# A hybrid trunk layer: residual of the FFN added during the up products, value norm on ScalarE, another product order in the first pass

## The chip, the cores and the metric

The kernel runs on one core of one Trainium2 chip. The metric is the device time of one execution in microseconds; the time before is 2174.49 us, the median of 3 runs (2174.28 to 2175.36). The core has five engines with instruction queues of their own: TensorE (PE in the profile; PEld is its load of weights), VectorE (DVE), ScalarE (ACT), GpSimd (POOL) and SyncE (SP), which only issues DMAs here. Every queue is worked off in order. ScalarE and POOL issue DMAs too.

## What is computed

One layer of depth 1 over 2048 tokens of 1024 features, all in float32:

```python
h   = x @ w_in                                   # u | v | queries
z   = gelu(h[..., :2048]);  u = z[..., :1024]
v   = layer_norm(z[..., 1024:], v_g, v_b)
mix = u * (einsum('gij,bnjgc->bnigc', w_m, v) + b_s)
branch = concat([mix, memory_cross_attention(queries, mem, w_mem_kv)])
x = layer_norm(ALPHA * x + branch @ w_o, ln1_g, ln1_b)
x = layer_norm(ALPHA * x + (silu(x @ w_1) * (x @ w_2)) @ w_down, ln2_g, ln2_b)
```

Here `ALPHA` is 2 to the power of 1/4 and the FFN is 2816 wide. The term `ALPHA * x` of the last line is the residual of the FFN; the norm of `v` over its 1024 features is the norm that the change speaks of.

## The kernel before

**Precision and products.** Every float32 operand is split into a hi part (ScalarE, CAST, L73) and a lo part (VectorE, subtraction, L74), and each product is three matmuls (hi·hi, hi·lo, lo·hi). Larger products are made by a scheme of seven half-size products instead of eight: the sums of weights that products 3, 5, 6 and 7 need are made on VectorE (L132, L133, L135, L136 in `halves`), while products 1, 2 and 4 take raw pieces of the weights. Products 1 and 2 add up in bank q0, 5 and 3 in q2, 7 and 4 in q3, and 6 stands alone in q1. A tuple `ORDER` (L342, `1, 6, 5, 7, 2, 3, 4`) says in which order they are made.

**Order of work.** Each matmul is tied to the one before it (`in_order`), so TensorE's order is the program's. The instructions of the other engines are placed by a scheduler, which follows the program's order but moves an instruction ahead of others where it expects it to be ready.

**Mixer, 0 to about 745 us.** Four chunks of 512 tokens. `v_half` makes the value half: its matmuls, GELU on ScalarE (L694) into two tiles `z[0]` and `z[1]` of 128 x 4 x 512, statistics, an inverse square root in small VectorE steps (L319 to L324, result `rs`), and the norm: eight VectorE instructions a chunk over 128x512 (L702), which subtract the mean and multiply by `rs`. The gating products `sg` (`mixed`, L788) take `z` as their stationary operand: `mixed(0)` and `mixed(1)` use `z[0]`, the others `z[1]`. In chunk 0 the keys and values of the memory (`memory_kv`) and the queries (`queries`, products named `q`, weights `w_q`) follow `v_half`; in the other chunks the first quarter of `u` (`u_half`, products named `u`, weights `w_u`, sums L711 and L715) and the reading of the memory follow it. The weight sums of `u` and `q` are made on POOL. The layer norm behind the mixer centres in L226, squares in L229, scales in L280 and finishes in L289, and for the last chunk it runs inside the first steps of the FFN.

**FFN, three passes of 688, 680 and 680 tokens.** A pass has 22 steps `f`, each 128 of the 2816 columns, in five blocks. A step (`up`) is seven products of 12 matmuls each, named `h`. Behind each product stands its stage: a copy `m` of q0 on ScalarE behind product 1, sums on VectorE behind 6, 5, 7, 3 and 4 (L399, L400, L401, L391, L395), Silu on ScalarE, and the gating multiplications (L396, L397). A list `work` of generators is advanced once behind each stage: this is how other work (a norm, the splits of `g`, the sums of the down weights) is spread over the steps. The steps of a block are followed by its down projection, which adds to the accumulators `fa` (`pa.ya`). In the first pass all sums of weights are made from raw weights and kept in DRAM; the later passes read them back. In passes 1 and 2 the down projections of blocks 0 to 3 are `down7`: 4 pairs of output tiles with 28 products in all, named `e`, whose sums on VectorE are L523, L530 and L531. In the last of these four (`last`), `down7` also fetches the residual: 16 loads of 170 KB from `x1d` on SP's queue (L538) and 16 VectorE instructions of 128x340 that add it (L540). The step behind it begins with its weight `r_u`, loaded by SP (L141), and the split of its first product's weight, `w1`.

Of the kernel before, what the change touches and what calls it, by code (L numbers as in the profile page):

```python
# [11 lines left out]
F32 = mybir.dt.float32  # L12
F32R = mybir.dt.float32r
AF = mybir.ActivationFunctionType
# [3 lines left out]
P = 128  # L18
# [21 lines left out]
def trunk_kernel(ctx, tc, xT, memT, wv, wuq, ws, bs, vg, vb, wmk, wmv, wo,  # L40
# [304 lines left out]
    class Pass:  # L345
# [38 lines left out]
        def up(self, f, work):  # L384
            no, h = self.no, self.h
            name = f"{no}_{f}"
            q0, q1, q2, q3 = banks = [bank(f"h{i}_{name}")[:, 0:h] for i in range(4)]
            m1, u2, c12, c21, c22 = (self.tmp(f"{x}_{f}") for x in ("m1", "u2", "c12", "c21", "c22"))

            def sum3():  # L390
                nc.vector.tensor_add(c12, q2, u2)  # L391
                nc.scalar.activation(c12, c12, AF.Silu)

            def sum4():
                nc.vector.tensor_add(c21, q3, u2)  # L395
                nc.vector.tensor_mul(c22, c22, c12)  # L396
                nc.vector.tensor_mul(c21, c21, m1)  # L397

            stages = {1: lambda: nc.scalar.copy(m1, q0), 6: lambda: nc.vector.tensor_add(u2, q1, m1),  # L399
                      2: lambda: nc.scalar.activation(m1, q0, AF.Silu), 5: lambda: nc.vector.tensor_add(c22, q2, u2),  # L400
                      7: lambda: nc.vector.tensor_add(c22, q3, c22), 3: sum3, 4: sum4}  # L401

            def then(stage):
                def run():
                    stage()
                    for gen, times in work:
                        for _ in range(times):
                            next(gen, None)
                return run

            wab = w1[f], w1[NF + f], f"u{name}"
            left = plain(*wab) if no else halves(*wab, nc.vector, False)
            products(left, lambda p, k, b: self.x[p][k][:, b], banks,
                     name, {p: then(stage) for p, stage in stages.items()}, ORDER, 0, key=f"u{f}")
            return c21, c22

        def whole(self, f, ys):
# [83 lines left out]
        def down7(self, blk, q, f0, last, w):  # L501
# [23 lines left out]
            def second(j):  # L525
                for p in (2, 3, 4):
                    product(j, p)
                if last:
                    y, u = self.out[j], self.u[j]
                    nc.vector.tensor_add(y[:, 0, h:n], y[:, 0, h:n], u)  # L530
                    nc.vector.tensor_tensor(out=y[:, 1].rearrange("p (b t) -> p b t", b=2),  # L531
                                            in0=y[:, 1].rearrange("p (b t) -> p b t", b=2),
                                            in1=u.unsqueeze(1).broadcast_to([P, 2, h]), op=ALU.add)
                    for m in range(2):
                        m0 = (2 * j + m) * P
                        for x in range(2):
                            r, t0 = self.tmp(f"r{m}{x}_{j}"), self.t0 + x * h
                            nc.sync.dma_start(out=r, in_=x1d[m0:m0 + P, t0:t0 + h])  # L538
                            to = y[:, m, x * h:(x + 1) * h]
                            nc.vector.scalar_tensor_tensor(out=to, in0=r, scalar=ALPHA, in1=to,  # L540
                                                           op0=ALU.mult, op1=ALU.add)

            for j in range(KD // 2):
                if j < KD // 2 - 1:
# [4 lines left out]
                if j:  # L549
                    second(j - 1)  # L550
            second(KD // 2 - 1)

        def sums(self):

# [65 lines left out]
    class Chunk:  # L620
# [44 lines left out]
        def v_half(self, hooks):  # L665
# [31 lines left out]
                nc.vector.bn_aggr(mv[:, b, :], st[:, b])  # L697
            nc.vector.tensor_scalar(mv[:, :, 1], mv[:, :, 1], EPS, None, ALU.add)
            inv_sqrt(rs, mv[:, :, 1], rt)
            for h in range(2):  # L700
                for b in range(4):
                    nc.vector.tensor_scalar(z[h][:, b], z[h][:, b], mv[:, b, 0:1], rs[:, b:b + 1],  # L702
                                            ALU.subtract, ALU.mult)

        def feature_major(self, a, t, name, act):

# [195 lines left out]
    def run(c):  # L902
# [5 lines left out]
        if c == 0:  # L908
            for j in range(2):
                at(1, j, lambda j=j: load_memory(j))  # L910
            ch.v_half(hooks)
            memory_kv()
            gating_constants()
            ch.queries()
# [22 lines left out]
        else:  # L937
# [14 lines left out]
            ch.read(1)  # L952
            for j in range(3):
                ch.mixed(j)
                ch.gate(j)
                ch.u_half(j + 1)
            ch.mixed(3)
# [21 lines left out]
    late.norm.squares = open_pools["sq"]  # L979
    ffn.rest()  # L980
    norm_work = norm_steps([late.norm], [late.store], 5, 5)
    sums_to_make = [(blk, m) for blk in range(4) for m in range(0, KD, 2)]
    for no in range(len(FPASSES)):
        pa, h, n = ffn, FPASSES[no] // 2, FPASSES[no]
# [5 lines left out]
        side = []  # L990

        def up(f):
            work = [(norm_work, 1), *side]
            if no == 0 and f > 4 and sums_to_make:
                blk, m = sums_to_make.pop(0)
                work.append((pa.left_sums(blk, m, 4 * blk, 2), 1))
            ys = f, pa.up(f, work)
            for gen, _ in work[1:]:
                for _ in gen:
                    pass  # L1000
            side.clear()
# [2 lines left out]
        for blk, nb in enumerate(blocks):  # L1004
# [9 lines left out]
            else:  # L1014
                gs = [pa.whole(*y) for y in ahead] + [pa.whole(*up(f)) for f in fs]
                ahead = [] if end else [up(f0 + nb)]
            seven = no and not end
            if seven:
                first = [pa.left(blk, 0, f0, nb // 2)]
            if blk == 0:  # L1020
# [2 lines left out]
                pa.sums()  # L1023
            if seven:
                pa.down7(blk, nb // 2, f0, blk == len(blocks) - 2, first)
            elif not end:
                pa.down(blk, gs, f0, whole, lambda ci, m: None)
            elif no < len(FPASSES) - 1:
# [92 lines left out]
```

## Time and profile before

| | |
|---|---|
| median of 3 runs | 2174.49 us (2174.28 to 2175.36) |
| the profiled execution | 2181.2 us |
| its span, first to last instruction | 2179.4 us |
| mean granted TensorE clock | 0.984 |
| mixer / pass 0 / pass 1 / pass 2 and tail | about 0–752 / 752–1240 / 1240–1696 / 1696–2179 us |
| HBM traffic over the span | 186 GB/s |

Times in the views are in us from the span's start; a row of the timeline is start, length, engine, line, operation, output<-inputs by the program's names, shape and count, and in square brackets the idle time before it with what ended it. The granted clock is a share of full speed. Rows of a source line give the shortest, median and longest instruction in ns.

### The profile page before, as it was taken

Reading aid. Unit: us, or ns where it says so; the run is one execution under the profiler, and the core shown is the slowest. Engines: PE = TensorE matmul, PEld = TensorE weight load, DVE = VectorE, ACT = ScalarE, POOL = GpSimd, SP = SyncE. Lnnn points to the kernel's source line nnn. Section 1 sums busy time; section 2 is a strip of 40 time slices with the busy share of each in tenths; the row PEclk is TensorE's granted clock in tenths of the full one; section 3 lists DMA queues with packets and bytes.
Section 4 is the critical chain, followed back from the end, with each engine's and each line's share of the span. In section 5 each row is a group of like instructions: output and inputs, shape, how many; then the busy total and the mean of one; then the engine's idle time right before and its main releaser. Section 6 shows DMA issues by size and latency. Waiting matters only on the chain.

```text
span 2179.4 us, 35121 instructions
## 1 busy us (share of the span) xinstructions
PE 2095.6 (96%) x12938; PEld 1988.5 (91%) x12938; DVE 1591.2 (73%) x3050; ACT 921.9 (42%) x1846; POOL 350.7 (16%) x318
## 2 busy tenths in 40 slices
PE   9899999999999989999999999999999999999896
PEld 7898788788888889999999999999999999999895
DVE  6986796798789886778777875656748656666656
ACT  5553653564474453334334354232224353223234
POOL 0413321331322220011010330000002310000002
PEclk9999999999999999999999999999999999999998
DMA  6233314234333557667666557666754576667652
GB/s 213 78 109 122 118 62 161 97 107 142 129 97 108 171 202 262 246 243 267 233 249 252 175 198 267 222 228 236 265 203 147 194 274 224 233 229 235 236 167 88
DMA packets 155276, 408.13 MB, mean 187 GB/s; under 512 B 15584, under 2 KB 42336, under 8 KB 155104
## 3 DMA queue, kind: packets, MB, share of 16 engines
q1 hardware_dynamic: 132672, 325.80, 44.6%
q10 hardware_dynamic: 12672, 46.14, 5.5%
q0 software_dynamic: 9760, 33.95, 4.4%
q8 instruction: 102, 1.67, 0.3%
q14 instruction: 70, 0.57, 0.1%
HBM read 326.13 MB, written 79.69 MB: 186 GB/s over the span
## 4 chain that ended last, share of the span: by engine, by line
PE 63%; DVE 18%; DMA 7%; issue 5%; ACT 4%; POOL 3%; ACTq 0%; DVEq 0%; POOLq 0%; SPq 0%
PE h L60 31%; PE d L60 10%; PE e L60 9%; PE v L60 5%; PE u L60 3%; DMA r_x<-in_xT 2%; PE y L60 2%; DVE w_o L74 1%; DVE w L74 1%; DMA r_es<-in_w 1%; DMA r_u<-in_w 1%; DVE x L74 1%; POOL s_b L233 1%; DMA r_f<-x1d 1%; DVE w_u L74 1%
## 5 line engine op out<-in xcount | busy, mean ns | idle before, releaser
L60 PE MATMUL h<-x,w 128*128 128x340 f32 (+1 forms) x5544 | 891.7, 322 | 33.7 <-DVE w L74 24.9
L60 PEld LDWEIGHTS h<-x,w 128*128 128x128 f32 x5544 | 880.2, 190 | 40.9 <-DVE w L74 27.9
L60 PE MATMUL d<-g,w_d 128*128 128x344 f32 (+3 forms) x1632 | 260.8, 320 | 2.7 <-DVE w_d L74 1.6
L60 PEld LDWEIGHTS d<-g,w_d 128*128 128x128 f32 x1632 | 256.5, 188 | 5.1 <-DVE w_d L74 2.2
L60 PE MATMUL y<-br,w_o 128*128 128x512 f32 x960 | 224.2, 395 | 0.0
L60 PEld LDWEIGHTS y<-br,w_o 128*128 128x128 f32 x960 | 180.5, 188 | 41.8
L60 PE MATMUL e<-gp,w_e 128*128 128x340 f32 x1344 | 210.8, 317 | 0.0
L60 PEld LDWEIGHTS e<-gp,w_e 128*128 128x128 f32 x1344 | 209.7, 188 | 0.0
L73 ACT CAST w<-r_u 128x512 fp32r<-128x512 f32 x198 | 122.5, 619 | 194.0 <-PE h L60 96.6
L60 PE MATMUL v<-w_v,x 128*128 128x512 f32 x768 | 188.7, 402 | 6.5 <-ACT w_v L73 4.8
L60 PEld LDWEIGHTS v<-w_v,x 128*128 128x128 f32 x768 | 144.5, 191 | 41.9 <-ACT w_v L73 4.8
L74 DVE TENSOR_TENSOR w<-r_u,w 128x512 fp32r<-128x512 f32 x198 | 138.5, 702 | 24.7 <-ACT w L73 17.7
L391 DVE TENSOR_TENSOR c<-h,u 128x340 f32<-128x340 f32 (+1 forms) x66 | 33.7, 511 | 97.3 <-PE h L60 97.0
L60 PE MATMUL u<-xt,w_u 128*128 128x256 f32 x768 | 98.0, 284 | 0.0
L60 PEld LDWEIGHTS u<-xt,w_u 128*128 128x128 f32 x768 | 95.1, 192 | 0.0
L60 PE MATMUL u<-x,w_u 128*128 128x256 f32 x576 | 79.2, 290 | 11.2 <-DVE u L711 6.7
L60 PEld LDWEIGHTS u<-x,w_u 128*128 128x128 f32 x576 | 72.8, 193 | 13.7 <-issue 6.2
L74 DVE TENSOR_TENSOR w_o<-r_o,w_o 128x512 fp32r<-128x512 f32 (+1 forms) x96 | 67.0, 706 | 21.3 <-ACT w_o L73 21.1
L523 DVE TENSOR_TENSOR fa<-fa,e 128x340 f32<-128x340 f32 x128 | 63.6, 505 | 23.7 <-PE e L60 21.7
L73 ACT CAST w_d<-r_d 128x384 fp32r<-128x384 f32 (+2 forms) x104 | 53.2, 519 | 65.3 <-PE d L60 41.0
L73 ACT CAST w<-s_u 128x512 fp32r<-128x512 f32 x88 | 54.0, 618 | 58.2 <-PE d L60 33.4
L73 ACT CAST w_e<-r_e 128x256 fp32r<-128x256 f32 x96 | 35.9, 404 | 99.4 <-PE e L60 77.3
(212 smaller groups left out, 2837.5 us busy)
## 6 DMA issues: line engine op xcount, KB each, us to landing
w<-k_u SPq DMA_DIRECT2D x176, 512.0 KB, 4.0
r_u<-in_w SPq DMA_DIRECT2D x88, 512.0 KB, 3.6
k_u<-w ACTq DMA_DIRECT2D x88, 512.0 KB, 3.8
r_u<-in_wuq SPq DMA_DIRECT2D x32, 512.0 KB, 3.3
r_o<-in_wo SPq DMA_DIRECT2D x32, 512.0 KB, 3.5
r_e<-in_w SPq DMA_DIRECT2D x64, 256.0 KB, 3.5
w_e<-k_e SPq DMA_DIRECT2D x64, 256.0 KB, 3.8
w_e<-k_e SPq DMA_DIRECT2D x32, 512.0 KB, 4.5
```

What stands on the lines that cost most here:

```text
L60: in_order(nc.tensor.matmul(*args, **kw))
L73: nc.scalar.copy(hi, src)
L74: engine.tensor_sub(lo, src, hi.bitcast(F32))
L233: nc.gpsimd.tensor_add(self.s2, self.s2, sq)
L391: nc.vector.tensor_add(c12, q2, u2)
L523: nc.vector.tensor_add(to, to, bk)
```

## The change

Three things are changed, and the number of matmuls is the same.

First, `down7` no longer loads and adds the residual. A new generator `residual()` does it while the steps of blocks 1 and 2 run: it takes two tiles of the pool `ln` in turn, issues a load on POOL's queue (170 KB, 16 in a pass), waits three stages a piece, and adds a tile six stages after its load was issued. Each add is tied behind the last stage sum on VectorE (`self.mark`). What is left is drained before block 3's down projection.

Second, the norm of `z` is an Identity activation on ScalarE with scale `rs` and bias `-mean * rs` (`zb`, one small VectorE instruction); `normal(0)` stands at the end of `v_half`, `normal(1)` right behind `v_half` in chunk 0 and behind `mixed(0)` in the others.

Third, the first pass makes its seven products in the order 1, 6, 2, 5, 7, 3, 4.

```diff
+            def add(out, x, y):
+                self.mark = nc.vector.tensor_add(out, x, y).ins
...
-                     name, {p: then(stage) for p, stage in stages.items()}, ORDER, 0, key=f"u{f}")
+                     name, {p: then(stage) for p, stage in stages.items()}, ORDER if no else (1, 6, 2, 5, 7, 3, 4), 0, key=f"u{f}")
...
-                    for m in range(2):
-                        m0 = (2 * j + m) * P
-                        for x in range(2):
-                            r, t0 = self.tmp(f"r{m}{x}_{j}"), self.t0 + x * h
-                            nc.sync.dma_start(out=r, in_=x1d[m0:m0 + P, t0:t0 + h])
-                            to = y[:, m, x * h:(x + 1) * h]
-                            nc.vector.scalar_tensor_tensor(out=to, in0=r, scalar=ALPHA, in1=to,
-                                                           op0=ALU.mult, op1=ALU.add)
...
+        def residual(self):
+            h, late = self.h, []
+            def add():
+                to, r = late.pop(0)
+                ins = nc.vector.scalar_tensor_tensor(out=to, in0=r, scalar=ALPHA, in1=to, op0=ALU.mult, op1=ALU.add)
+                tc.add_manual_dep(ins.ins, self.mark.name, ...)
+            for m in range(KD):
+                for x in range(2):
+                    if len(late) == 2:
+                        add()
+                    r = open_pools["ln"].tile([P, 432], F32, tag=f"s{1 + x}", name=f"res{self.no}_{m}_{x}")[:, 0:h]
+                    t0 = self.t0 + x * h
+                    nc.gpsimd.dma_start(out=r, in_=x1d[m * P:(m + 1) * P, t0:t0 + h])
+                    late.append((self.ya[m][:, x * h:(x + 1) * h], r))
+                    for _ in range(3):
+                        yield
+            while late:
+                add()
+                for _ in range(3):
+                    yield
...
-            for h in range(2):
-                for b in range(4):
-                    nc.vector.tensor_scalar(z[h][:, b], z[h][:, b], mv[:, b, 0:1], rs[:, b:b + 1],
-                                            ALU.subtract, ALU.mult)
+            self.zs, self.zb = rs, common.tile([P, 4], F32, tag="zb", name=f"zb{c}")
+            nc.vector.scalar_tensor_tensor(out=self.zb, in0=mv[:, :, 0], scalar=-1.0, in1=rs,
+                                           op0=ALU.mult, op1=ALU.mult)
+            self.normal(0)
+
+        def normal(self, h):
+            for b in range(4):
+                z = self.z[h][:, b]
+                nc.scalar.activation(z, z, AF.Identity, scale=self.zs[:, b:b + 1], bias=self.zb[:, b:b + 1])
...
-            work = [(norm_work, 1), *side]
+            work = [(norm_work, 1), (residual, 1), *side]
...
+            if blk == 3:
+                for _ in residual:
+                    pass
...
             if seven:
                 pa.down7(blk, nb // 2, f0, blk == len(blocks) - 2, first)
+                if blk == 0:
+                    residual = pa.residual()
```

On VectorE, at the end of the last `down7` of pass 1, the row before stands as follows (`e0` to `e3` are the banks of its products, `fa` and `fu` the accumulators, `g1_16` the operand of the next down projection, `w1_1_17` the lo part of the weight of product 1 of the next step):

```order
L531 TENSOR_TENSOR fa1_4_13479<-fa1_4_13479,fu1_4_13483 128x680
L540 SCALAR_TENSOR_TENSOR fa1_4_13479<-r01_2_1_16202,fa1_4_13479 128x340
...
L523 TENSOR_TENSOR fa1_6_13480<-fa1_6_13480,e3_1_3_3_16147 128x340
L530 TENSOR_TENSOR fa1_6_13480<-fa1_6_13480,fu1_6_13484 128x340
L531 TENSOR_TENSOR fa1_6_13480<-fa1_6_13480,fu1_6_13484 128x680
L540 SCALAR_TENSOR_TENSOR fa1_6_13480<-r00_3_1_16234,fa1_6_13480 128x340
...
L74 TENSOR_TENSOR g1_16_16246<-c21_16_1_15779,g1_16_16246 128x340
L74 TENSOR_TENSOR w1_1_17_16264<-r_u1_17_0_16260,w1_1_17_16264 128x512
```

In the changed kernel the same place reads (L526, L533 and L534 are the former L523, L530 and L531):

```order
L74 TENSOR_TENSOR g1_16_16254<-c21_16_1_15835,g1_16_16254 128x340
L74 TENSOR_TENSOR w1_1_17_16272<-r_u1_17_0_16268,w1_1_17_16272 128x512
L526 TENSOR_TENSOR fa1_6_13488<-fa1_6_13488,e3_1_3_3_16179 128x340
L526 TENSOR_TENSOR fa1_4_13487<-fa1_4_13487,e0_1_3_2_16121 128x340
...
L534 TENSOR_TENSOR fa1_4_13487<-fa1_4_13487,fu1_4_13491 128x680
L526 TENSOR_TENSOR fa1_6_13488<-fa1_6_13488,e0_1_3_3_16176 128x340
...
L534 TENSOR_TENSOR fa1_6_13488<-fa1_6_13488,fu1_6_13492 128x680
L391 TENSOR_TENSOR u2_17_1_16264<-h1_1_17_16260,m17_1_16263 128x340
```

The residual's adds are gone from here, and the lo part of `w1` stands in front of the last sums instead of behind them.

On ScalarE, in chunk 0, behind the first cast of the query weights the row before is this (`r_q` are raw weights, `s_q` sums of them, `vz` the values of the memory):

```order
L73 CAST w_q_657<-r_q_0_648 128x512
L73 CAST w_q_674<-s_q_653 128x512
L73 CAST w_q_690<-s_q_652 128x512
L73 CAST w_q_706<-r_q_1_649 128x512
L73 CAST vz<-vp_551 128x2x64
```

In the changed kernel it is:

```order
L73 CAST w_q_659<-r_q_0_650 128x512
L732 ACTIVATE z_0_297<-z_0_297,zb_473,rs_107 128x512 x4
L732 ACTIVATE z_1_448<-z_1_448,zb_473,rs_107 128x512 x4
L73 CAST vz<-vp_553 128x2x64
L73 CAST vz<-vp_554 128x2x64
L73 CAST w_q_676<-s_q_655 128x512
```

All eight activations of the norm stand between the first and the second cast of `w_q`.

On VectorE, in step 1 of the first pass (`w5_0_1` is the lo part of the weight of product 5 of step 1, `y0_3` to `y3_3` the tiles that the late norm centres), the row before is:

```order
L132 TENSOR_TENSOR s1_u0_2_7757<-r_u0_2_1_7754 128x512
L391 TENSOR_TENSOR c12_0_0_7419<-h2_0_0_7415,u2_0_0_7418 128x344
L226 SCALAR_TENSOR_TENSOR y0_3_6902<-mean_a3_7539,y0_3_6902 128x512 x2
...
L226 SCALAR_TENSOR_TENSOR y3_3_7296<-mean_a3_7539,y3_3_7296 128x512 x2
L74 TENSOR_TENSOR w5_0_1_7650<-s1_u0_1_7592,w5_0_1_7650 128x512
L74 TENSOR_TENSOR w7_0_1_7668<-s3_u0_1_7596,w7_0_1_7668 128x512
L74 TENSOR_TENSOR w2_0_1_7686<-r_u0_1_0_7588,w2_0_1_7686 128x512
```

In the changed kernel it is (the stage sums all have the line of their helper, L391):

```order
L391 TENSOR_TENSOR c12_0_0_7427<-h2_0_0_7423,u2_0_0_7426 128x344
L74 TENSOR_TENSOR w2_0_1_7658<-r_u0_1_0_7596,w2_0_1_7658 128x512
L226 SCALAR_TENSOR_TENSOR y0_3_6910<-mean_a3_7547,y0_3_6910 128x512 x2
...
L226 SCALAR_TENSOR_TENSOR y3_3_7304<-mean_a3_7547,y3_3_7304 128x512 x2
L74 TENSOR_TENSOR w5_0_1_7674<-s1_u0_1_7600,w5_0_1_7674 128x512
L74 TENSOR_TENSOR w7_0_1_7692<-s3_u0_1_7604,w7_0_1_7692 128x512
...
L132 TENSOR_TENSOR s1_u0_2_7765<-r_u0_2_1_7762 128x512
```

The lo part of `w2` now stands in front of the eight instructions L226, that of `w5` still behind them, and L132 of the next step has moved behind both.

More of the change, by code (lines that the diff above doesn't have):

```diff
@@ L388, in up @@
             m1, u2, c12, c21, c22 = (self.tmp(f"{x}_{f}") for x in ("m1", "u2", "c12", "c21", "c22"))
+            def add(out, x, y):
+                self.mark = nc.vector.tensor_add(out, x, y).ins
             def sum3():
-                nc.vector.tensor_add(c12, q2, u2)
+                add(c12, q2, u2)
                 nc.scalar.activation(c12, c12, AF.Silu)
             def sum4():
-                nc.vector.tensor_add(c21, q3, u2)
+                add(c21, q3, u2)
                 nc.vector.tensor_mul(c22, c22, c12)
                 nc.vector.tensor_mul(c21, c21, m1)
-            stages = {1: lambda: nc.scalar.copy(m1, q0), 6: lambda: nc.vector.tensor_add(u2, q1, m1),
-                      2: lambda: nc.scalar.activation(m1, q0, AF.Silu), 5: lambda: nc.vector.tensor_add(c22, q2, u2),
-                      7: lambda: nc.vector.tensor_add(c22, q3, c22), 3: sum3, 4: sum4}
+            stages = {1: lambda: nc.scalar.copy(m1, q0), 6: lambda: add(u2, q1, m1),
+                      2: lambda: nc.scalar.activation(m1, q0, AF.Silu), 5: lambda: add(c22, q2, u2),
+                      7: lambda: add(c22, q3, c22), 3: sum3, 4: sum4}
             def then(stage):
@@ L551, in down7 @@
             second(KD // 2 - 1)
+        def residual(self):
[3 more added lines that the diff above has]
+                ins = nc.vector.scalar_tensor_tensor(out=to, in0=r, scalar=ALPHA, in1=to, op0=ALU.mult, op1=ALU.add)
+                tc.add_manual_dep(ins.ins, self.mark.name,
+                                  mybir.DependencyInfo(mybir.DependencyClass.NoSync, mybir.DependencyReason.DATA),
+                                  reason="order of VectorE")
+            for m in range(KD):
[12 more added lines that the diff above has]
+                    yield
         def sums(self):
@@ L911, in run @@
             ch.v_half(hooks)
+            ch.normal(1)
             memory_kv()
@@ L954, in run @@
                 ch.mixed(j)
+                if j == 0:
+                    ch.normal(1)
                 ch.gate(j)
@@ L981, in trunk_kernel @@
     norm_work = norm_steps([late.norm], [late.store], 5, 5)
+    residual = iter(())
     sums_to_make = [(blk, m) for blk in range(4) for m in range(0, KD, 2)]
@@ L997, in up @@
             ys = f, pa.up(f, work)
-            for gen, _ in work[1:]:
+            for gen, _ in work[2:]:
                 for _ in gen:
```

## The prediction, made before the run

> **What bounds the kernel now.** The first thing read is the page: which engine is busy, and by whom the chain that ended last was held.
>
> ```profile
> PE 2095.6 (96%) x12938; PEld 1988.5 (91%) x12938; DVE 1591.2 (73%) x3050; ACT 921.9 (42%) x1846; POOL 350.7 (16%) x318
> PE 63%; DVE 18%; DMA 7%; issue 5%; ACT 4%; POOL 3%; ACTq 0%; DVEq 0%; POOLq 0%; SPq 0%
> ```
>
> TensorE is the bound, and the change leaves its products alone: only idle time and slowly clocked time can go. The second view is what TensorE waits for (us in total, times, longest).
>
> ```profile
> PE h L60 <- DVE w L74: 24.9, 9, 6.5
> ...
> PE sg L60 <- DVE z L702: 4.0, 5, 0.9
> ```
>
> The up products `h` wait for a lo half of a weight that VectorE subtracts in L74, and the gating products `sg` for the norm of the v half. The third view is the windows view: the end of the last seven-product block of pass 1, the FFN step of 84 matmuls behind it, the next step, the same stretch of pass 2, and two more stretches of use below. The last three figures of a row are the granted clock, the DMA share and GB/s.
>
> ```profile
> 1552.00:1576.10 24.10, 24.10 (x158) 24.10 (x157) 22.15 (x50) 4.43 (x11) 0.00 (x0) 1.00 0.91 288
> 1576.10:1597.80 21.70, 16.13 (x86) 15.85 (x86) 10.52 (x21) 3.35 (x7) 0.00 (x0) 0.84 0.58 210
> 1597.80:1610.80 13.00, 13.00 (x85) 13.00 (x84) 6.36 (x12) 4.03 (x9) 0.00 (x0) 1.00 0.65 219
> 2030.50:2052.00 21.50, 15.96 (x86) 15.68 (x86) 10.49 (x21) 3.34 (x7) 0.00 (x0) 0.84 0.58 206
> 475.80:479.00 3.20, 3.20 (x16) 3.20 (x16) 3.20 (x8) 0.42 (x1) 0.00 (x0) 0.50 0.00 0
> 776.00:782.80 6.80, 4.07 (x14) 4.08 (x15) 6.80 (x8) 2.30 (x4) 5.11 (x4) 0.50 0.38 154
> ```
>
> The same 84 matmuls take 13.00 us at a full clock, and 21.70 and 21.50 us behind the block: 8.7 and 8.5 us too long. In the first of them 5.57 us (21.70 − 16.13) is idle, and 3.13 us (16.13 − 13.00) is the price of the clock of 0.84. So a stall here costs about one and a half times its own length.
>
> **The residual.** The timeline shows who made that stall (start, us, engine, line).
>
> ```profile
> 1575.12 1.35 DVE L540 SCALAR_TENSOR_TENSOR fa<-r,fa 128x340 f32<-128x340 f32 x3
> ...
> 1578.85 1.77 DVE L540 SCALAR_TENSOR_TENSOR fa<-r,fa 128x340 f32<-128x340 f32 x4
> ...
> 1581.39 1.28 DVE L74 TENSOR_TENSOR w<-r_u,w 128x512 fp32r<-128x512 f32 x2
> 1582.12 8.06 PEld L60 LDWEIGHTS h<-x,w 128*128 128x128 f32 x34 [5.85 <-DVE w L74]
> ```
>
> The lo half that TensorE waits for (1581.39) stands last in VectorE's queue, behind the block's sums and the residual adds L540. In the changed order there is no L540 here, and that lo half stands in front of the last evictions. The 16 small loads of a pass also leave SP's queue, where the weight of this step is issued behind them. Removed: 8.7 + 8.5 = 17.2 us at most. I take 16.5 and leave 0.35 us a pass for a lo half that still comes a little late; the low end is 10, where a shorter stall and half of the slow clock stay.
>
> What is added are 16 loads on POOL's queue and 16 adds on VectorE a pass, inside the up steps of blocks 1 and 2. Rows on these steps, on the add, and on loads of this size (KB, median us to landing):
>
> ```profile
> 1442.70 28.49 PE L60 MATMUL h<-x,w 128*128 128x340 f32 x182
> 1451.17 0.51 DVE L400 TENSOR_TENSOR c<-h,u 128x340 f32<-128x340 f32 x1 [0.53 <-PE h L60]
> ...
> L540 DVE SCALAR_TENSOR_TENSOR fa<-r,fa x32: 501/504/512, 1559.3 to 2034.5; 128x340 f32<-128x340 f32 x32
> ...
> r_es<-in_w POOLq DMA_DIRECT2D x32, 256.0 KB, 5.7
> ...
> fa<-x1d SPq DMA_DIRECT2D x4, 688.0 KB, 10.5
> ...
> x1d<-y POOLq DMA_DIRECT2D x4, 512.0 KB, 6.8
> ```
>
> TensorE runs 182 matmuls there without a gap. A product is 13.00 / 7 = 1.86 us. VectorE's sum of product 5 (L400) waits for its product and is over 0.51 us after the release; product 3, which reuses that bank, comes two products (3.7 us) after product 5. So about 3.1 us are free behind each such sum, and one add of 0.50 us fits: I cost 32 adds at nothing. Were that cover gone, they would cost 32 × 0.50 = 16 us, the whole gain of this part. The add is queued in order, so it also waits for its load, and the next stage sums wait behind it. It stands six stages behind its issue, 6 × 1.86 = 11.2 us; with the 3.1 us it harms only if a load takes over 14.3 us. The loads on POOL's queue take 5.7 to 6.8 us (medians, 256 to 512 KB), the slowest load from `x1d` has a median of 10.5; 170 KB is nearest to the first, so nothing.
>
> The Trainium skill, "SBUF — State Buffer", section "Who interferes with whom", speaks against this move: a DMA of GpSimd's queue can starve for descriptors while VectorE runs an instruction in a two-port mode, one of ScalarE's or SyncE's queue cannot. By it the 16 loads would be safer where they were; the rows above show no starving at 5.7 us, in a stretch where VectorE is busy.
>
> **The norm of the v half.** Per chunk eight L702 leave VectorE and eight activations come onto ScalarE; the nearest row for these is L289, an identity with scale and bias columns at the same 128x512.
>
> ```profile
> L702 DVE TENSOR_SCALAR z<-z,mv,rs x32: 532/540/1576, 62.1 to 659.4; 128x512 f32<-128x512 f32 x32
> ...
> L289 ACT ACTIVATE y<-y,l1b,l1g x32: 797/802/820, 261.1 to 816.5; 128x512 f32<-128x512 f32 x32
> ...
> 470.70 6.57 DVE L702 TENSOR_SCALAR z<-z,mv,rs 128x512 f32<-128x512 f32 x8
> ...
> 473.63 0.49 PE L60 MATMUL sg<-wm,z 128*128 128x128 f32 x2 [0.85 <-DVE z L702]
> ...
> 475.03 2.93 PE L60 MATMUL sg<-wm,z 128*128 128x128 f32 x12 [0.92 <-DVE z L702]
> ...
> 488.21 1.95 PE L60 MATMUL sg<-wm,z 128*128 128x128 f32 x16
> ...
> PE u L60 <- DVE w_u L74: 1.6, 1, 1.6
> PE u L60 <- DVE u L715: 0.6, 1, 0.6
> ...
> PE sg L60 <- DVE z L702: 1.8, 2, 0.9
> PE u L60 <- DVE u L711: 1.2, 1, 1.2
> ```
>
> Of the four waits at the end, the first two are of chunk 1 (280 to 320 us), the last two of chunk 3 (645 to 690 us). In chunk 2 eight L702 take 6.57 us, since POOL works beside them, and the first 16 `sg` matmuls end at 477.96: 5.6 us from 472.39, where 16 undisturbed ones take 1.95. Part of the loss is the half clock from 475.8. On ScalarE the first four tiles, which alone these `sg` need, start about 0.74 us apart and end at about 470.85 + 3 × 0.74 + 0.80 = 473.9; `sg` is through near 475. Gain 3. In chunk 1 `sg` gains nothing by that sum, but VectorE is free 4 us earlier and the two waits of `u` (1.6 + 0.6) go: 2. In chunk 3 both kinds are there (1.8 and 1.2), of which I take 2. Chunk 0 pays:
>
> ```profile
> 60.12 0.62 ACT L73 CAST w_q<-s_q 128x512 fp32r<-128x512 f32 x1 [0.59 <-issue]
> ...
> 61.87 0.16 DVE L324 SCALAR_TENSOR_TENSOR rs<-rt,rs 128x4 f32<-128x4 f32 x1
> ...
> 68.09 4.40 PE L60 MATMUL q<-xt,w_q 128*128 128x256 f32 x36
> ```
>
> There all eight activations stand ahead of the casts of `w_q` in ScalarE's queue, and they wait for `rs` (62.03). They end near 62.2 + 7 × 0.74 + 0.80 = 68.2, the cast and its lo half near 70.2, where TensorE wants them from 68.09: 2.1 us lost. The sum is −3 − 2 − 2 + 2 = −5; between −9 (chunk 0 covered, chunk 2's slow clock gone too) and +3 (chunk 0 draws a slow stretch, and ScalarE holds up others).
>
> The Trainium skill, "ScalarE: Activation LUTs", "Rules for kernel authors", says to put adds and multiplications on VectorE and not on ScalarE. The rows agree while POOL is quiet (540 against 802 ns) and not beside POOL (up to 1576 ns). By the rule alone this term would be eight times 0.26 us a chunk against the change, about +8.
>
> **The order in the first pass.** Product 2, whose weight is a raw piece that needs no sums, comes third instead of fifth.
>
> ```profile
> 752.48 6.15 PE L60 MATMUL h<-x,w 128*128 128x344 f32 x38
> ...
> 776.34 1.27 DVE L226 SCALAR_TENSOR_TENSOR y<-mean_a,y 128x512 f32<-128x512 f32 x2
> 777.53 2.82 DVE L74 TENSOR_TENSOR w<-s_u,w 128x512 fp32r<-128x512 f32 x2
> 778.73 13.11 PE L60 MATMUL h<-x,w 128*128 128x344 f32 x70 [6.52 <-DVE w L74]
> ...
> 827.52 0.44 ACT L399 COPY m<-h 128x344 f32<-128x344 f32 x1
> ...
> 828.53 0.94 PE L60 MATMUL h<-x,w 128*128 128x344 f32 x2 [3.32 <-ACT w L73]
> ...
> L399 ACT COPY m<-h x22: 433/441/451, 757.8 to 1188.7; 128x344 f32<-128x344 f32 x22
> ```
>
> In step 1 the lo half of product 5 stands behind eight L226 of the late norm; TensorE loses 6.5 us, and the window 776 to 782.8 runs at a clock of 0.50. In the changed order the lo half of product 2 stands ahead of the L226, so that 1.9 us of work lies in the gap; about 4 us of 6.5 go (an L132 that waits for a load also moves behind them), and with them some of the 3.4 us that the slow window costs. I take −5.5. Against it, product 2 adds to the bank that ScalarE's copy `m` reads, and now follows that copy after one product instead of three. In step 4 the copy comes at 827.5, when TensorE already stands: +1. In the other steps a sum per bank gets one product of cover less or more: 0 ± 4. Together −4.5, from −9 to +4.
>
> **Sum.** −16.5 − 5 − 4.5 = −26.0 against the profiled execution's 2181.2 us, whose span is 2179.4: 2155.2. The runs have a median of 2174.49, 6.7 us (0.3%) below that execution; the same loss on it gives 2148.5.
>
> **Rivals.** *The first pass gives back.* In step 0 product 1 is over near 752.48 + 1.9 = 754.4 and the copy starts only at 757.8: 3.4 us late, against the 1.9 us that product 6 covers. If that holds for the first six steps, which share ScalarE with the late norm, 6 × 1.5 = 9 us are lost, the gain in step 1 falls to 3, and the part is +6 instead of −4.5: 2159. For it: ScalarE works in order. Against it: it is the norm's work that makes the copy late, and that is over after step 4. *The stall at the block's end only shrinks.* If the weight's load or cast is next in line, a wait of 2.8 us and a slow stretch worth 1.7 stay in each pass: the gain there is 2 × 4.1 = 8.2 and the time 2157. For it: the DMA engines are taken to 0.91 in the 24 us ahead of it (row from 1552), and the weight is loaded there. Against it: 16 loads of 170 KB fewer are in that stretch. *ScalarE's norm loses.* With chunk 0 at +4.3 and little won in the others the norm is +3 and the time 2156.5. *The other side, slower: the loads on POOL's queue come late.* VectorE stands at each add until its load is there. From 14.3 us to landing it costs; at 14.3 + 26/32 = 15.1 us the gain is eaten; at 16 us the 32 adds cost 32 × 1.7 = 54 us, and the time is 2203. For it: the two tiles allow only two loads ahead, and the same 0.91 at a block's end. Against it: 5.7 to 6.8 us in this queue, half of what is allowed. The page on SBUF named above, of the Trainium skill, would be its mechanism.
>
> **How the numbers follow.** My forecast has a chance of 0.60, the first pass giving back 0.15, the stall that only shrinks 0.12, the norm that loses 0.08, late loads 0.05. The range is 2138 to 2166: below, all three parts at their good ends (17.2 + 9 + 9 = 35, 2139); above, the first two rivals together (−8.2 − 5 + 6 = −7, 2167). A change of 0.2% (4.3 us) is what a measurement of this kernel can tell from none. All cases but late loads lie beyond it on the fast side, and some of them could fall together: faster 0.91, same 0.04, slower 0.05.
>
> **What would show it.** In the profile after, no wait of 5.6 us and no clock of 0.84 behind the fourth block of passes 1 and 2, so that a step there takes 13 to 13.7 us; residual adds without idle time before them that ends by a DMA; `sg` of chunk 2 through in under 3 us, and a new wait of about 2 us for a `w_q` in chunk 0; the wait at 772 down to about 2 us. I am wrong if the loads take over 14 us, or if `h` waits for the copy in ScalarE in many steps of the first pass.

## The result, and the profile after

The changed kernel takes 2153.68 us (median of 4 runs, 2150.82 to 2157.44), against 2174.93 for the kernel before in runs beside it. The ratio is 0.9903, with a 95% interval of 0.9890 to 0.9917: 21 us or 1.0% faster, where the prediction had 26 us and a time of 2148.5. The profiled execution took 2155.43 us, its span 2153.7, against 2181.2 and 2179.4 before, so its own difference is 25.7 us. Where these lie shows best in four stages, cut in the trace where the first `h` product of passes 0 and 1 starts and where the last matmul ends (us; the parts alone are runs told below):

| stage | before | after | residual alone | norm alone | order alone |
|---|---|---|---|---|---|
| mixer | 752.5 | 744.3 | 752.3 | 745.9 | 752.7 |
| pass 0 | 487.4 | 489.2 | 486.8 | 481.6 | 488.1 |
| passes 1 and 2 | 928.5 | 912.8 | 912.7 | 926.7 | 926.8 |
| tail | 11.0 | 7.4 | 7.3 | 11.0 | 11.0 |
| span | 2179.4 | 2153.7 | 2159.2 | 2165.2 | 2178.6 |

The mixer gained 8.2 us, passes 1 and 2 15.7, the tail 3.6, and the first pass lost 1.8. The rows are of one execution each, and the first pass varies most: with the old order in all its steps it took 481.6 to 487.4 us in five of the kernels of this document, with the new one 486.5 to 489.2 in six. The waits of TensorE show the trade (us in total, times, longest):

```profile
PE h L60 <- ACT m L402: 9.2, 4, 5.9
PE h L60 <- DVE c L391: 8.5, 7, 1.9
...
PE h L60 <- DVE w L74: 4.2, 3, 1.8
PE q L60 <- DVE w_q L74: 3.2, 2, 2.9
...
PE sg L60 <- ACT z L732: 1.7, 8, 0.2
```

The waits for a lo half of a weight are down from 24.9 to 4.2 us, and those for the norm of z from 4.0 to 1.7. Two others stand in their place: `h` waits for the copy `m` of its bank on ScalarE, and for VectorE's sums out of its banks.

**The residual.** The stretches that answer to the 21.70 and 21.50 us of before, in the windows view:

```profile
1571.40:1584.50 13.10, 13.10 (x86) 13.10 (x86) 6.14 (x11) 3.35 (x7) 0.00 (x0) 1.00 0.70 249
2017.40:2030.50 13.10, 13.10 (x86) 13.10 (x86) 6.13 (x11) 3.36 (x7) 0.00 (x0) 1.00 0.73 241
```

TensorE is busy throughout, at a full clock. The timeline has the lo half where the order said, ahead of the last sums, and it is done before the products `e` of the block are:

```profile
1565.93 0.68 DVE L74 TENSOR_TENSOR w<-r_u,w 128x512 fp32r<-128x512 f32 x1
1566.53 0.92 DVE L526 TENSOR_TENSOR fa<-fa,e 128x340 f32<-128x340 f32 x2
...
1571.38 1.88 PE L60 MATMUL h<-x,w 128*128 128x340 f32 x11
```

The new loads and adds, from the list of DMA issues (KB, median us to landing), and from the timeline of a step in block 1 of pass 1:

```profile
res<-x1d POOLq DMA_DIRECT2D x32, 170.0 KB, 3.9
```

```profile
1354.90 0.50 DVE L391 TENSOR_TENSOR c<-h,u 128x340 f32<-128x340 f32 x1
1355.32 0.50 DVE L556 SCALAR_TENSOR_TENSOR fa<-res,fa 128x340 f32<-128x340 f32 x1
1355.74 0.50 DVE L74 TENSOR_TENSOR gp<-c,gp 128x340 fp32r<-128x340 f32 x1
```

A load lands in 3.9 us (median; the slowest in 6.2), and the add stands between a stage sum and a split with no idle time before it. The same holds of all 32 adds.

**The norm.** The first `sg` products of chunk 2, which took from 472.39 to 477.96 before, and the query products of chunk 0:

```profile
469.66 0.49 PE L60 MATMUL sg<-wm,z 128*128 128x128 f32 x2 [0.22 <-ACT z L732]
...
471.78 1.38 PE L60 MATMUL sg<-wm,z 128*128 128x128 f32 x10 [0.22 <-ACT z L732]
...
68.59 0.50 PE L60 MATMUL q<-xt,w_q 128*128 128x256 f32 x2 [1.51 <-ACT w_q L73]
71.98 5.83 PE L60 MATMUL q<-xt,w_q 128*128 128x256 f32 x34 [2.89 <-DVE w_q L74]
```

The gating products are through 3.5 us after they start instead of 5.6 (the prediction had under 3), in small steps of one activation each. In chunk 0 TensorE stands 4.4 us for the second weight of the queries, as the prediction had it but twice as long, and part of it is regained later.

**The first pass.** Step 4, by the timeline:

```profile
818.91 0.69 DVE L132 TENSOR_TENSOR s_u<-r_u 128x512 f32<-128x512 f32 x1 [6.78 <-DMA r_u<-in_w]
819.52 0.51 DVE L400 TENSOR_TENSOR c<-c,m 128x344 f32<-128x344 f32 x1
...
820.07 0.48 ACT L73 CAST g<-c 128x344 fp32r<-128x344 f32 x1 [8.01 <-DVE c L400]
820.45 0.44 ACT L402 COPY m<-h 128x344 f32<-128x344 f32 x1
820.94 15.23 PE L60 MATMUL h<-x,w 128*128 128x344 f32 x79 [5.88 <-ACT m L402]
```

This is a chain through three engines. VectorE stands in order at a weight sum (L132) whose load is late; behind it waits the multiplication L400; for that waits ScalarE's cast of `g`; behind the cast, in ScalarE's order, stands the copy `m`; and product 2, now third, needs the copy. In the kernel before, the load of the same weight was late too and cost 3.3 us of TensorE's time. There product 2 comes fifth; the first to wait was product 7, the fourth, for the cast of its weight, which stands behind the same copy. Now the wait is 5.9 us. Not all of the difference is the order's distance: the weight sum L132 was over 7.3 us after the first product of the step had started in the kernel before and 8.5 us after it here, since the load took 10.7 us to land instead of 9.5.

### The profile page after: what moved, and what is told of

Its sections match the earlier page's. It is cut to its first block, busy times and chain, and to the rows that moved or that the text cites. A ratio compares the mean times of both kernels' runs of the same rounds, so it can differ in the third digit from the quotient of the medians.

```text
span 2153.7 us, 35119 instructions
## 1 busy us (share of the span) xinstructions
PE 2088.3 (97%) x12938; PEld 1980.6 (92%) x12938; DVE 1573.3 (73%) x3022; ACT 944.0 (44%) x1878; POOL 366.7 (17%) x350
## 4 chain that ended last, share of the span: by engine, by line
PE 65%; DVE 15%; DMA 8%; ACT 5%; issue 4%; POOL 3%; SPq 0%; ACTq 0%; DVEq 0%; POOLq 0%
PE h L60 32%; PE e L60 10%; PE d L60 10%; PE v L60 6%; PE u L60 4%; DMA r_x<-in_xT 2%; DMA r_es<-in_w 2%; DVE w_o L74 2%; POOL s_b L233 1%; DMA r_f<-x1d 1%; DVE w L74 1%; PE y L60 1%; POOL s_a L233 1%; DVE x L74 1%; ACT p L774 1%
## 5 line engine op out<-in xcount | busy, mean ns | idle before, releaser
L60 PE MATMUL h<-x,w 128*128 128x340 f32 (+1 forms) x5544 | 884.9, 321 | 24.9 <-ACT m L402 9.2
L391 DVE TENSOR_TENSOR c<-h,u 128x340 f32<-128x340 f32 (+1 forms) x198 | 100.8, 509 | 120.7 <-PE h L60 119.9
L403 ACT ACTIVATE m<-h 128x340 f32<-128x340 f32 (+1 forms) x66 | 30.0, 455 | 126.9 <-PE h L60 123.6
L74 DVE TENSOR_TENSOR w_o<-r_o,w_o 128x512 fp32r<-128x512 f32 (+1 forms) x96 | 69.5, 733 | 22.0 <-ACT w_o L73 21.9
L526 DVE TENSOR_TENSOR fa<-fa,e 128x340 f32<-128x340 f32 x128 | 64.6, 506 | 25.8 <-PE e L60 23.6
```

The source lines that it names most:

```text
L60: in_order(nc.tensor.matmul(*args, **kw))
L74: engine.tensor_sub(lo, src, hi.bitcast(F32))
L391: self.mark = nc.vector.tensor_add(out, x, y).ins
L526: nc.vector.tensor_add(to, to, bk)
```

## The experiments

Twelve kernels were run. Ratios are to the kernel before, in runs on the same chip, with 95% intervals.

### The three parts alone

Each of these three kernels has one part of the change and not the other two. Where these runs speak of steps 22 to 65, steps are counted through all passes, 22 a pass: step 39 is the one behind the fourth block of pass 1, step 61 that of pass 2. The residual alone is the changed kernel with these edits (the two calls of `normal(1)` and the bias `zb` go too):

```diff
-                     ..., ORDER if no else (1, 6, 2, 5, 7, 3, 4), 0, key=f"u{f}")
+                     ..., ORDER, 0, key=f"u{f}")
-            self.normal(0)
+            for h in range(2):
+                for b in range(4):
+                    nc.vector.tensor_scalar(z[h][:, b], z[h][:, b], mv[:, b, 0:1], rs[:, b:b + 1],
+                                            ALU.subtract, ALU.mult)
```

> The kernel before, with the residual's move alone. Theory A (the two stalls behind the fourth block go whole, the adds in blocks 1 and 2 cost nothing): steps 39 and 61 take 13.1 us instead of 21.7 and 21.5, every other stretch of passes 1 and 2 stays within 0.5 us, and the ratio to before is 0.992 (17 us less). Theory B (VectorE's adds or the loads on POOL's queue cost up to 0.1 us each): 14 us less, with the difference lying in blocks 1 and 2, a ratio of 0.9935.

Measured: 2158.94 us, 0.9910 (0.9893 to 0.9926). Steps 39 and 61 take 13.1 us, 8.6 and 8.4 less than before, and in blocks 1 and 2 TensorE waits for nothing, as before the change. So theory A holds on the two stalls and on the adds. Two things were not in it: the tail is 3.6 us shorter, and the down projection of block 0 in pass 1 takes 27.1 us instead of 25.9.

The norm of z alone is the kernel before with this one:

```diff
-            for h in range(2):
-                for b in range(4):
-                    nc.vector.tensor_scalar(z[h][:, b], z[h][:, b], mv[:, b, 0:1], rs[:, b:b + 1],
-                                            ALU.subtract, ALU.mult)
+            self.normal(0)                      # and normal(1) where the changed kernel has it
```

> The kernel before, with the norm of z on ScalarE alone. If the mixer's gain in the changed kernel is that norm's: chunk 0 ends 1.5 to 2 us later, chunk 1 5 us, chunks 2 and 3 2 to 3 us each earlier, the mixer ends about 8 us earlier, the time is about 2167. The prediction's size of it was -5 (2169.5). A rival: with the old order the late norm's stall in step 1 takes part of it back, 2170 or more.

Measured: 2170.87 us, 0.9968 (0.9955 to 0.9981), 7 us less; the mixer ends 6.6 us earlier, with 3.1 us lost by the end of the queries of chunk 0. That is between the prediction's 5 and the 8.2 of the changed kernel. The two `u` stretches of chunk 1 give the most, 2.6 and 2.8 us: the second of them the prediction had left as it was.

The order alone is the kernel before with

```diff
-                     ..., ORDER, 0, key=f"u{f}")
+                     ..., ORDER if no else (1, 6, 2, 5, 7, 3, 4), 0, key=f"u{f}")
```

> The kernel before, with the product order of the first pass alone. Theory A (the order itself costs: product 2 must wait for ScalarE's copy of its bank, and products 3 and 4 for VectorE's sum of theirs, one product earlier than before): the first pass takes 1 to 3 us more than before, the time is about 2176 to 2178, and the profile shows waits of h for the copy m of 6 to 9 us in all. Theory B (the order gains what the prediction said, and the other two parts spoil it by shifting the first pass): the first pass takes 4 to 5 us less, the time is about 2170.

Measured: 2181.04 us, 1.0018 (1.0008 to 1.0027): slower by 4 us, from 2 to 6. Theory A holds. The profiled execution shows only 0.7 us of it in the first pass (488.1 against 487.4), because step 17 was slow in the kernel before (see below). Its waits in the first pass are of the kind and size of the changed kernel's:

```profile
PE h L60 <- ACT m L399: 7.8, 3, 4.3
PE h L60 <- DVE c L400: 6.2, 5, 1.9
```

By their ratios the three parts alone sum to −19.6 − 7.0 + 3.9 = −22.7 us, against −21.1 together. Each has an uncertainty of 2 to 4 us, so it does not show whether the parts act on one another.

### The order, taken back whole and by half

The changed kernel with the old order in all passes:

```diff
-                     ..., ORDER if no else (1, 6, 2, 5, 7, 3, 4), 0, key=f"u{f}")
+                     ..., ORDER, 0, key=f"u{f}")
```

> The changed kernel with the product order of before in all passes. Theory A: about 2 us less than the changed kernel, some 2151.5, with the wait for the lo half behind the late norm back in step 1 (about 6.5 us and a slow stretch), and no wait for the copy m in step 4. Theory B: about 4.5 us more than the changed kernel, 2158.

Measured: 2151.26 us, 0.9877 (0.9864 to 0.9890): below the changed kernel, whose interval (0.9890 to 0.9917, in other runs) begins where this one ends. Its first pass takes 484.4 us against 489.2. In step 1 the old stall is back in full, and in step 4 product 7 waits 2.3 us for a cast where product 2 had waited 5.9 for the copy:

```profile
772.55 12.57 PE L60 MATMUL h<-x,w 128*128 128x344 f32 x70 [7.57 <-DVE w L74]
...
821.66 0.58 PE L60 MATMUL h<-x,w 128*128 128x344 f32 x2 [2.34 <-ACT w L73]
```

With a third order instead:

```diff
-                     ..., ORDER if no else (1, 6, 2, 5, 7, 3, 4), 0, key=f"u{f}")
+                     ..., ORDER if no else (1, 6, 5, 2, 7, 3, 4), 0, key=f"u{f}")
```

> The changed kernel with the order 1, 6, 5, 2, 7, 3, 4 in the first pass: the copy m gets two products of cover instead of one (three before), the sum behind product 5 two instead of one, the sum behind product 7 one as in the changed kernel. Theory A: the waits for m in steps 0 and 4 shrink by 1.9 us each and those of product 3 for its bank go (about 4 us in steps 8, 9, 13, 17), while the gain in step 1 goes too, since product 5 is again ahead of product 2 (some 2 us back): 2 to 4 us less than the changed kernel, 2150 to 2152. Theory B: half of the order's gain, 2156.

Measured: 2152.14 us, 0.9878 (0.9862 to 0.9894), the first pass 483.6 us. In the first pass the waits for `m` fall from 8.9 to 0.9 us; those for the sums only from 5.9 to 4.0, while the sum behind product 7 still has one product of cover. In step 0, where both kernels wait for the copy, the wait is 0.5 us with two products of cover and 1.6 with one; and the waits of steps 8 and 9 for the bank of product 3 (0.6 and 1.5 us) are gone, with two products of cover for that bank too. There the loss is shown to be one of the distances between products which share a bank. Step 4 (15.0 us instead of 21.9) shows nothing of the kind: here the weight sum L132 stands behind the multiplication L400 in VectorE's queue, in the changed kernel ahead of it, so the chain told above is not there.

### The norm of chunk 0 on VectorE

```diff
+            if c == 0:
+                for h in range(2):
+                    for b in range(4):
+                        nc.vector.tensor_scalar(z[h][:, b], z[h][:, b], mv[:, b, 0:1], rs[:, b:b + 1],
+                                                ALU.subtract, ALU.mult)
+                return
...
-            ch.normal(1)
             memory_kv()
```

> The changed kernel with the norm of z in chunk 0 on VectorE as before, in chunks 1 to 3 on ScalarE. Theory A: the wait for the query weights (4 us of which 1.7 are left at the end of chunk 0) was made by the eight activations that stand ahead of their casts: q takes 12.9 us instead of 16.8, and the time is 1.5 to 2 us below the changed kernel's. Theory B: chunk 0 is bound elsewhere by its end and the loss is made up by then: no difference over 0.5 us.

Measured: 2152.74 us, 0.9878 (0.9859 to 0.9896). The wait of 4.4 us in the queries is gone:

```profile
66.45 1.45 PE L60 MATMUL q<-x,w_q 128*128 128x256 f32 x10 [0.58 <-DVE w_q L74]
67.73 4.47 PE L60 MATMUL q<-xt,w_q 128*128 128x256 f32 x36
```

That the eight activations made it is shown. The whole mixer is only 1.0 us shorter than in the changed kernel (743.3 against 744.3), and the times of the two are not told apart. Over all the traces the loss in chunk 0 is plain: chunk 1's first value product starts at 217.3 to 218.5 us in the seven kernels with these eight activations and at 214.8 to 215.9 in the seven without.

### How much the adds are covered

To the changed kernel one more VectorE instruction is added ahead of each residual add.

```diff
+                wide = nc.vector.reduce_max(whole[:, 344:408], r[:, 0:64].unsqueeze(2).broadcast_to([P, 64, 32]), axis=AX.X)
```

> The changed kernel with one more VectorE instruction ahead of each of the 32 residual adds, a reduction over 128x64x32 that writes an unused corner of the tile (about 2.1 us). It stands for a residual that holds VectorE 2 us longer. Theory A (about 3.1 us of VectorE's time are free behind each stage sum, as the prediction has it): 2.1 + 0.5 us fit, the ratio stays at 0.990. Theory B (the splits of the operands of the down projection already use that time): 0.5 to 1 us each, a ratio of 0.998 to 1.005.

Measured: 2186.94 us, 1.0038 (1.0023 to 1.0053).

With 80 in place of 32:

> As wide_2us, with a reduction over 128x64x80 (about 5.3 us). Theory A: what lies over 3.1 us is paid, (5.3 + 0.5 - 3.1) x 32 = 86 us, 2240, somewhat more where a slow clock follows the stalls. Theory B: nearly all of it is paid, 5.3 x 32 = 170 us, 2320. If much less than 60 us is paid, the cover is larger than the prediction took it to be.

Measured: 2291.44 us, 1.0522 (1.0504 to 1.0539). The instruction itself, in the one kernel and in the other, and the wait of TensorE that it makes in the second:

```profile
L557 DVE TENSOR_REDUCE res<-res x32: 2272/2276/2280, 1352.2 to 1933.0; 128x64 f32<-128x2048 f32 x32
```

```profile
L557 DVE TENSOR_REDUCE res<-res x32: 5470/5474/5478, 1349.6 to 2031.1; 128x64 f32<-128x5120 f32 x32
```

```profile
PE h L60 <- DVE w L74: 96.4, 17, 11.7
```

Passes 1 and 2 take 940.9 and 1045.6 us against 912.8: 28.1 and 132.8 us more, or on average 0.88 us for each 2.28 us and 4.15 us for each 5.47 us, the slow clock behind the stalls included. Between the two every microsecond is paid (3.27 for 3.19), so what is free beside an add is on average 2.28 − 0.88 = 1.4 us, not the 2.6 that the prediction's 3.1 us leave. Theory B is nearer. The row shows what TensorE waits for: not the bank that the prediction looked at, but the lo half of the next weight, which stands behind the add in VectorE's queue.

The average hides how this is paid. With the shorter instruction, TensorE's waits in blocks 1 and 2 of pass 1 are these, for 16 adds:

```profile
PE h L60 <- DVE w L74: 10.0, 4, 3.8
```

The windows view has step 28 (three adds) and step 33 (two adds), first in the changed kernel, then with the shorter instruction. The first figure behind the window is its length, and the figures behind that are the busy times of TensorE, of its weight loads and of VectorE:

```profile
1348.96:1362.05 13.09, 13.09 (x87) 13.09 (x86) 10.14 (x22) 5.51 (x12) 1.59 (x3) 1.00 0.74 230
1440.59:1453.66 13.07, 13.07 (x86) 13.07 (x85) 7.72 (x16) 4.26 (x9) 1.07 (x2) 1.00 0.80 251
```

```profile
1351.39:1369.17 17.78, 13.98 (x86) 13.70 (x85) 16.44 (x25) 5.50 (x12) 1.67 (x3) 0.96 0.70 208
1452.75:1465.83 13.08, 13.08 (x86) 13.08 (x85) 11.70 (x18) 4.27 (x9) 1.08 (x2) 1.00 0.69 213
```

In the changed kernel VectorE has 3.0 us free in step 28, and 4.7 us are paid there for three instructions of 2.28 us; it has 5.4 us free in step 33, and nothing is paid for two. Of the seven steps with adds in this pass, the four with 3.0 to 3.2 us free pay 1.3 to 4.7 us, and the three with 5.2 to 7.1 us free pay 0 to 0.9. So the cover is not a fixed time behind each sum; the steps fit a cover that is what VectorE's queue has free over the whole step.

### Looking for a better version

Two more kernels: the changed one with the new order in step 1 alone and chunk 0's norm on VectorE (`best`), and the same with the four accumulator loads tied behind step 4 in SP's queue (`best_fa`).

```diff
+                     ..., (1, 6, 2, 5, 7, 3, 4) if no == 0 and f == 1 else ORDER, 0, key=f"u{f}")
...
+                    tc.add_manual_dep(ins.ins, self.late.name, ...)     # the load of fa, behind step 4
```

> The changed kernel with the new product order in step 1 of the first pass alone (the old one in its other steps), and the norm of z of chunk 0 on VectorE. Theory A (the order pays in step 1, where the late norm stands ahead of the lo half, and costs in the other steps): 2.4 us less in step 1 and 1.7 us less in chunk 0 than the kernel with the old order, which was at 0.9877 of before: 0.986. Theory B: step 1 loses with its copy m what it gains, and chunk 0 makes it up by its end: 0.9877.

Measured: 2151.60 us, 0.9872 (0.9855 to 0.9889). The gain in step 1 did not come; its waits of 7.6 us with the old order are 6.6 with the new one:

```profile
766.69 0.59 PE L60 MATMUL h<-x,w 128*128 128x344 f32 x2 [2.33 <-ACT m L402]
771.56 12.81 PE L60 MATMUL h<-x,w 128*128 128x344 f32 x70 [4.28 <-DVE w L74]
```

> The kernel best with one more edit: the four loads of the accumulators from x1d (688 KB each) are placed behind step 4 in SP's queue instead of right behind the weights of step 5. Theory A (the stall of step 4 in every kernel so far comes from the weight of step 5, which lands 10.7 us after its issue because those 2.75 MB are moved at the same time, and on which VectorE stands in order): step 4 takes 14 us instead of 18 to 20, some 4 us less than best, 0.984. Theory B (the stores of x1d and the loads for the sums ahead of it are enough to make it late): step 4 stays over 17 us and the time is that of best.

Measured: 2148.10 us, 0.9864 (0.9844 to 0.9884). Step 4 takes 13.2 us, as theory A had it, but the time is not told apart from `best`, where it took 14.7 without this edit. The same edit on the changed kernel, with its order and its chunk 0:

> The changed kernel with the four accumulator loads behind step 4 in SP's queue, its product order kept. Theory A (the copy m of step 4 is late only because ScalarE stands behind a cast that waits for VectorE, and VectorE stands at the weight sum of step 5, whose load shares the DMA engines with the accumulators): the wait of 5.9 us for m in step 4 goes, step 4 takes 14 us instead of 21.9, and the time is 6 to 8 us under the changed kernel's, a ratio of 0.987. Theory B (the copy is late by the order alone): step 4 stays over 18 us, and the ratio is 0.990.

Measured: 2155.19 us, 0.9896 (0.9881 to 0.9911): no change beyond the uncertainty. Step 4 takes 19.0 us and VectorE still waits 5.2 us, though the accumulator loads are issued only at 833.4:

```profile
820.10 0.69 DVE L132 TENSOR_TENSOR s_u<-r_u 128x512 f32<-128x512 f32 x1 [5.17 <-DMA r_u<-in_w]
```

The loads of these weights, from the view of that tile between 790 and 840 us:

```profile
DMA to landing us min/median/max: 4.1/4.6/10.3
```

The slowest of these weight loads still needs 10.3 us (10.7 in the changed kernel), and 8.2 us in `best_fa` against 8.3 in `best`, so my theory that the accumulators make it late falls. What is left in those microseconds are the four stores of `x1d` and two loads for the sums on POOL's queue and the stores of weight sums on ScalarE's; that they are the cause was not tried. Nor was why this load took 10.0 to 10.7 us in the six kernels that have the new order in step 4, and 7.9 to 9.5 us in the eight others.

Last, the three edits together, each as shown above: the old order in all steps, chunk 0's norm on VectorE and the accumulators behind step 4.

> The changed kernel with the old product order in all steps, the norm of z of chunk 0 on VectorE and the accumulator loads behind step 4: what the runs point to. Theory A (the gains add up): 4 us in step 4 and 1.7 in chunk 0 on the kernel with the old order (0.9877): 0.985. Theory B (step 1 with its stall of 8 to 9 us keeps the first pass as long, or step 3 takes back what step 4 gives, as it did in best_fa): 0.987.

Measured: 2147.81 us, 0.9865 (0.9850 to 0.9880). It is 1.35% under the kernel before. Its interval is clear of the changed kernel's (0.9890 to 0.9917), which comes from other runs, and of that of `fa_behind` (0.9881 to 0.9911), which was run beside it. Step 4 still takes 17.4 us, though the load took 7.9 us here and 8.2 in `best_fa`. The difference is in VectorE's queue, here and then in `best_fa`:

```profile
815.84 0.69 DVE L132 TENSOR_TENSOR s_u<-r_u 128x512 f32<-128x512 f32 x1 [3.96 <-DMA r_u<-in_w]
816.45 0.51 DVE L400 TENSOR_TENSOR c<-c,m 128x344 f32<-128x344 f32 x1
```

```profile
815.33 0.51 DVE L400 TENSOR_TENSOR c<-c,m 128x344 f32<-128x344 f32 x1
...
817.82 0.69 DVE L132 TENSOR_TENSOR s_u<-r_u 128x512 f32<-128x512 f32 x1 [0.35 <-DMA r_u<-in_w]
```

The scheduler placed the weight sum that waits for the load behind the multiplication L400 in `best_fa`, so that the copy on ScalarE did not have to wait for the load. It did the same in `best` and with the third order, and in these three kernels step 4 takes 13.2 to 15.0 us; in the eleven others the weight sum stands ahead of that multiplication, and step 4 takes 17.4 to 21.9. No run ties this place alone. From the changed kernel's order taken back alone (0.9877) the last kernel is not told apart.

## Why the prediction was right or wrong, point by point

- **The residual: right in size and mechanism.** Predicted −16.5; the two stretches gave 8.6 + 8.4 = 17.0, both the idle time and the slow clock (passes 1 and 2 are 15.7 us shorter; the difference came back for the most part in the down projections of block 0; why is open). Added on top, unforeseen, was the tail's 3.6.
- **Its cover: right in outcome, wrong in size.** The adds cost nothing, but the cover is on average 1.4 us beside the add (1.9 with it), not 3.1. The step that failed is "about 3.1 us are free behind each such sum": it counted only the products until the same bank is used again, and neither the weight split that stands next in VectorE's queue nor how little of VectorE's time some steps leave free (3.0 us in step 28, for three adds).
- **Late loads on POOL's queue: did not occur.** 3.9 us to landing, against 14.3 us allowed. The Trainium skill, "SBUF — State Buffer", "Who interferes with whom", ties the starving of descriptors to VectorE's two-port instructions. In these two blocks VectorE ran only instructions of the kinds TENSOR_TENSOR and SCALAR_TENSOR_TENSOR, and that any of them runs in such a mode no run here shows, so the 3.9 us speak neither for nor against the rule.
- **The norm: right in sign, too small.** −5 was predicted; −8.2 shows in the changed kernel and −6.6 alone. Chunk 0 lost about what was said once it had ended (1.7 us against 2; the starts of chunk 1 told above differ by 1.4 to 3.7). The term that was mis-sized is chunk 1: its two `u` stretches gave 2.6 and 3.0, of which the prediction had 2 in all. What the Trainium skill, "ScalarE: Activation LUTs", "Rules for kernel authors", would make of it by its rule, 8 us slower by the prediction's estimate, did not come: ScalarE is busy for 44% of the span in the changed kernel, and TensorE's new waits on this account are 1.7 us for `z` in all and 4.4 us in chunk 0.
- **The first pass: wrong in sign.** −4.5 was predicted; the order costs about 4 us (1.0018 alone; 489.2 against 484.4 us of the first pass with and without it in the changed kernel; 488.1 against 487.4 in the kernel before). It is the outcome of the first rival, which had 0.15; that rival looked for late copies in the first six steps, and TensorE waits for the copy in steps 0, 1 and 4. Two sentences failed. "About 4 us of 6.5 go" in step 1: the 6.5 us became three waits of 4.4 us together, for the copy `m` (1.5), a lo half (1.1) and a bank's sum (1.9), and the step gained 1.9 us in the changed kernel and next to nothing in `best`. The slow window there was also taken too high: its row has TensorE busy for 4.07 us at half the clock, which costs 2.0 us, not 3.4. And "+1" for step 4 and "0 ± 4" for the others: step 4 lost 2.3 us and step 3 1.4, and steps 8, 13 and 14 lost 0.8 to 0.9 each, the first two at a bank's sum with one product of cover less, step 14 at the cast of a weight.
- **The 3.0 us that step 17 of the first pass gained need not be the order's.** In the kernel before it took 17.3 us in the profiled execution, with a wait of 2.4 us for one of VectorE's sums, which stood behind a sum of weights whose load VectorE awaited for 4.6 us; with the norm alone, in the old order, it took 13.5.

The sum itself: between the profiled executions' spans 25.7 us went, where the steps had 26.0, but by errors that cancel: 6.3 us too good in the first pass and 0.8 in passes 1 and 2, 3.2 us too bad in the mixer, and 3.6 of the tail that were in no step. That the sum of the steps came out is therefore luck; the residual's term, the largest, is not. In the medians 21.2 us went. The profiled execution of before was 6.3 us above the median beside the changed kernel (2174.93), that of the changed kernel 1.8 above its own, so a loss read from one execution came out 4.5 us smaller in the medians.

## What to carry to other kernels

When the order of products that share banks is changed, count for each bank how many products lie between the one that leaves a result in it and the next that touches it, and compare that with the latest, not the usual, lateness of the engine that empties it. An engine's queue in order carries a late load through other engines: follow the chain (load, VectorE, ScalarE, bank) before calling a copy cheap, and see whether the instruction that waits for the load can stand behind the ones that others need. And the cover of an added instruction ends at whatever is queued behind it, so look at the next few instructions on that engine and at what the engine has free over the step, not at the buffer it belongs to.

## What the runs showed of the hardware that was not expected

The end of the program went together with how POOL's DMA queue was used. In the kernel before and then in the changed one, the closing instructions of POOL's queue are:

```profile
L1117 POOLq DRAIN x3: 40/93/8214, 2170.5 to 2179.2; - x3
```

```profile
L1155 POOLq DRAIN x3: 40/93/3064, 2148.3 to 2153.4; - x3
```

The longest of POOL's closing drains takes 8.2 us in the three kernels without the 32 residual loads on its queue and 3.1 us in the eleven with them; the tail is 11.0 us in all of the former and 7.3 to 7.5 us in all of the latter. The two groups differ in more than the number of DMAs on that queue (92 and 124): the last of them is issued at 1755 to 1767 us in the former and at 1883 to 2021 us in the latter, and the residual's loads are on SP's queue in the former alone. Which of these makes the drain shorter, and why, is open.
